# Softmax statistics and joining coefficients of a dilated attention layer: by way of DRAM in place of TensorE

## The chip, the cores and the metric

The kernel runs on one core of one Trainium2 chip. The metric is the device time of one execution in microseconds (us). The kernel before was timed three times: median 1245.1 us, lowest 1243.75, highest 1247.14. One further execution was profiled and took 1243.98 us, of which the profile's span covers 1242.2 us. TensorE is PE below, VectorE DVE, ScalarE ACT, GpSimd POOL, and SyncE, which issues most transfers, SP.

## The reference

A trunk of two layers over 512 tokens of width 1024. Layer A (sparse attention and memory attention, then an MLP) is untouched. In layer B each of 8 heads attends three times over shared keys and values, in windows (128, step 1), (512, step 4) and (2048, step 16), and the three results are merged by their softmax denominators:

```python
for gi, (window, dil) in enumerate(DIL_PATTERNS):
    n_k = window // dil + 1
    idx = t[:, None] - dil * jnp.arange(n_k)[None, :]
    s = jnp.einsum('bhqd,bhqkd->bhqk', q_b[:, gi], k_g).astype(jnp.float32) * scale
    s = jnp.where(valid, s, NEG)
    lse = jax.nn.logsumexp(s, axis=-1, keepdims=True)
    p = jnp.exp(s - lse)
    outs.append(jnp.einsum('bhqk,bhqkd->bhqd', p.astype(v.dtype), v_g))
    lses.append(lse)
wts = jax.nn.softmax(jnp.stack(lses), axis=0).astype(v.dtype)
return jnp.sum(jnp.stack(outs) * wts, axis=0)
```

The result goes through an output projection and an MLP to the output.

## The kernel before, in words

The heads are worked on in four pairs (`sp` 0 to 3, pair 0 to pair 3 below). For each pair `proj_b` makes the queries: products of 128x384 in float32r, three to a term (lines 275, 279 and 280, helper `mm3`), since each operand is split into a high part and a remainder. The weights come by a transfer into `st`, ACT copies the high part into `w` (line 268), DVE subtracts for the remainder (line 270); line 275 multiplies by the high part, line 279 by the remainder. `attn_b` then has two rounds `w`. Round 0 is the local window (step 1), with queries in natural order. Round 1 is the two dilated windows together (steps 4 and 16), with queries sorted by residue modulo 4. In each round the scores (line 790) go to PSUM, DVE adds the mask and takes the running minimum of the negated scores (line 754, "mask" below), ACT takes the exponential (line 231), PE turns the probabilities (lines 1676 and 1685), and PE multiplies them with the values (line 771; `close0` ends round 0, `close1` round 1). Both write their 128x512 result to the one PSUM bank of pool `po`. `close0` copies it away in residue order (line 1703, ACT); the result `O1` of `close1` stays in the bank until `norm_b` has read it, so `close0` of the next pair waits for that.

`norm_b` joins the two rounds. The statistics of a round are, for each token and head, a minimum and a sum: `st0` (round 0) and `st1` (round 1), tiles of 128 x 4 blocks x 4 numbers. `st0` has tokens in natural order and must be brought into residue order. Before, PE turns its four blocks to 4x512 (line 1725), DVE copies that with the permutation (line 1727), PE turns it back (line 1731), and DVE copies it out (line 1733). A short chain of DVE operations and one exponential make the coefficients `cc`, two for each token and head. They must be spread from one number for a token and head to 64 partitions: DVE splits them (lines 315 and 316), PE turns them to 8x512 (line 1755), DVE copies (line 1759), and PE spreads them by two products with a matrix `sel` of ones (lines 1763 and 1768). ACT copies one of the two out (line 1765), DVE multiplies (lines 1766 and 1769), adds (line 1770) and splits the sum for the output projection (lines 1774 and 1775).

What sets the order: `norm_b` is a generator in a side queue; each `yield` hands one step of `attend`, which puts one item of attention work and some projection work between, and the counts NY, NZ (before: 6 and 0) say how many steps to pause. A scheduler then fixes the order on each engine from this sequence; each engine works strictly in that order, and an instruction that waits holds all behind it. The same holds for the order in which SP issues transfers.

## Time and profile before

| | |
|---|---|
| median of 3 runs | 1245.1 us (1243.75 to 1247.14) |
| profiled execution | 1243.98 us, span 1242.2 us |
| busy, share of the span | PE 1221.2 us (98%), DVE 821.2 (66%), ACT 720.5 (58%), POOL 331.0 (27%) |
| attention of layer B, with its side work | about 727 to 895 us of the span |
| first and last instruction of line 1725 (start of `norm_b` on PE) | 770.7 and 864.4 us |
| last product with `sel` (line 1768) | 880.1 us |

In rows of a timeline the columns are start and duration in us, engine, line, operation, output and inputs, and count; a bracket gives the idle time just before and what ended it. Matmuls are pipelined: the duration of one overlaps the next, so the time that one takes from PE is read from start to start.

### The profile page before, as it was taken

The page shows a single profiled execution, that of the slowest core. Times are in us where ns is not written, and L with a number is a line of the kernel's source. Part 1 is how long each engine was busy: PE and PEld are TensorE (multiplying, and loading weights), DVE is VectorE, ACT ScalarE, POOL GpSimd, SP SyncE. Part 2 cuts the span into 40 slices and gives each one's busy share as a digit, 9 for nine tenths or more (in the row PEclk, how much of TensorE's full clock was granted, in tenths as well). Part 3 has the DMA queues.
Part 4 walks back from the last instruction along what each step waited for, and adds up shares of the span by engine and source line. Part 5 has one row for each costly group of instructions (what it writes and reads, how often), then busy time and mean ns, then how long its engine had stood idle before and what let it go on. Part 6 is the DMA issues. An engine that isn't in the chain of part 4 may idle for free.

```text
span 1242.2 us, 17962 instructions
## 1 busy us (share of the span) xinstructions
PE 1221.2 (98%) x6307; PEld 998.0 (80%) x6307; DVE 821.2 (66%) x1531; ACT 720.5 (58%) x1579; POOL 331.0 (27%) x418
## 2 busy tenths in 40 slices
PE   9999999999999999999999999999999999999998
PEld 7768877787788888888888898877688888888887
DVE  7857676764567557566589566777766747557466
ACT  6834678874476464553557446667666455364462
POOL 4535864731040000000001767642241000000000
PEclk9999999999999999999999999999999999999999
DMA  7531232342498797896976342211379698697634
GB/s 272 203 107 44 96 109 94 89 115 84 131 273 235 227 274 224 266 246 216 275 218 200 97 130 61 70 39 41 124 220 267 212 274 248 200 295 220 170 109 162
DMA packets 62219, 215.41 MB, mean 173 GB/s; under 512 B 6929, under 2 KB 15313, under 8 KB 61617
## 3 DMA queue, kind: packets, MB, share of 16 engines
q1 hardware_dynamic: 50656, 143.69, 35.4%
q0 software_dynamic: 9728, 35.93, 14.8%
q10 hardware_dynamic: 1744, 34.63, 7.5%
q8 instruction: 50, 0.82, 0.3%
q14 instruction: 41, 0.33, 0.1%
HBM read 208.89 MB, written 72.35 MB: 226 GB/s over the span
## 4 chain that ended last, share of the span: by engine, by line
PE 72%; ACT 5%; DVE 5%; POOL 2%; issue 2%; DMA 2%; ACTq 0%; DVEq 0%; POOLq 0%
PE s_ps L275 13%; PE s_ps L279 13%; PE s_ps L280 13%; PE s_acc L275 5%; PE s_acc L280 5%; PE s_acc L279 5%; PE s_pt L280 3%; PE s_pt L275 3%; PE s_pt L279 3%; PE s_po L771 3%; ACT s_p L231 1%; PE s_ps L790 1%; DVE s_w L270 1%; ACT s_pt L767 1%; ACT s_w L268 1%
## 5 line engine op out<-in xcount | busy, mean ns | idle before, releaser
L270 DVE TENSOR_TENSOR s_w<-s_st,s_w 128x1024 fp32r<-128x1024 f32 (+3 forms) x254 | 295.9, 1171 | 252.8 <-ACT s_w L268 252.3
L268 ACT ACTIVATE s_w<-s_st 128x1024 fp32r<-128x1024 f32 (+4 forms) x260 | 251.4, 973 | 211.3 <-PE s_pt L280 54.7
L275 PE MATMUL s_ps<-s_act,s_w 128*128 128x512 f32 x560 | 218.6, 392 | 1.0 <-ACT s_act L313 0.7
L279 PE MATMUL s_ps<-s_act,s_w 128*128 128x512 f32 x560 | 218.3, 390 | 0.0
L280 PE MATMUL s_ps<-s_act,s_w 128*128 128x512 f32 x560 | 218.1, 390 | 0.0
L1238 POOL DMA_DIRECT2D sum<-sum x16 | 14.2, 887 | 430.8 <-ACT s_p L231 430.8
L275 PEld LDWEIGHTS s_ps<-s_act,s_w 128*128 128x128 f32 x560 | 104.9, 188 | 24.0 <-ACT s_act L313 2.0
L279 PEld LDWEIGHTS s_ps<-s_act,s_w 128*128 128x128 f32 x560 | 105.2, 188 | 22.1 <-DVE s_act L316 0.4
L280 PEld LDWEIGHTS s_ps<-s_act,s_w 128*128 128x128 f32 x560 | 105.1, 188 | 21.8
L275 PE MATMUL s_acc<-s_w,s_act 128*128 128x512 f32 (+3 forms) x288 | 102.1, 359 | 2.1 <-ACT s_act L294 0.7
L279 PE MATMUL s_acc<-s_w,s_act 128*128 128x512 f32 (+3 forms) x288 | 101.4, 354 | 0.0
L280 PE MATMUL s_acc<-s_w,s_act 128*128 128x512 f32 (+3 forms) x288 | 99.5, 351 | 0.0
L231 ACT ACTIVATE s_p<-s_ps 128x512 f32<-128x512 f32 x64 | 38.0, 594 | 89.1 <-PE s_ps L280 86.3
L759 POOL TENSOR_SCALAR s_p<-s_p,s_cr,s_ab 128x128 f32<-128x128 f32 (+3 forms) x96 | 61.0, 661 | 58.8 <-DVE s_cr L1127 39.2
L231 ACT ACTIVATE s_p<-s_ps,s_nm 128x256 f32<-128x256 f32 (+3 forms) x128 | 65.8, 528 | 16.0 <-PE s_pt L1145 4.5
L767 ACT ACTIVATE s_pt<-s_pt 128x512 f32<-128x512 f32 (+2 forms) x99 | 51.5, 528 | 20.6 <-PE s_pt L1676 7.3
L275 PEld LDWEIGHTS s_acc<-s_w,s_act 128*128 128x128 f32 x288 | 54.2, 188 | 10.3 <-issue 1.7
L313 ACT ACTIVATE s_qk<-s_p 128x256 fp32r<-128x256 f32 (+1 forms) x96 | 46.9, 489 | 21.2 <-DVE s_p L1248 19.4
L279 PEld LDWEIGHTS s_acc<-s_w,s_act 128*128 128x128 f32 x288 | 54.4, 189 | 4.2 <-issue 0.2
L280 PEld LDWEIGHTS s_acc<-s_w,s_act 128*128 128x128 f32 x288 | 54.1, 189 | 4.4
L316 DVE TENSOR_TENSOR s_qk<-s_p,s_qk 128x256 fp32r<-128x256 f32 (+1 forms) x96 | 50.9, 530 | 0.0
L279 PE MATMUL s_acc<-s_w,s_qk 128*128 128x512 f32 x128 | 49.9, 390 | 0.0
(329 smaller groups left out, 2724.6 us busy)
## 6 DMA issues: line engine op xcount, KB each, us to landing
s_st<-in_w_up_dram SPq DMA_DIRECT2D x64, 512.0 KB, 4.3
s_st<-sum SPq DMA_DIRECT2D x64, 512.0 KB, 6.1
s_st<-in_w_db_dram SPq DMA_DIRECT2D x48, 512.0 KB, 4.4
sum<-in_w_db_dram POOLq DMA_DIRECT2D x16, 1024.0 KB, 14.2
sum<-sum POOLq DMA_DIRECT2D x16, 1024.0 KB, 11.2
s_st<-in_w_bq_dram SPq DMA_DIRECT2D x16, 384.0 KB, 3.4
s_st<-in_w_ag_dram SPq DMA_DIRECT2D x11, 512.0 KB, 3.6
s_w<-in_w_c_dram SPq DMA_DIRECT2D x8, 512.0 KB, 4.7
```

Of the source, the lines that this page charges most:

```text
L231: return lambda *a, **k: self.marks.append(f(*a, **k))
L268: nc.scalar.activation(w[:, 0], st, AF.Copy)
L270: e.tensor_tensor(out=w[:, 1], in0=st, in1=w[:, 0], op=ALU.subtract)
L275: m = mm(ps, lh[0], rh[0], start=start, stop=False, skip_group_check=again)
L279: mm(ps, lh[0], rh[1], start=False, stop=False, skip_group_check=again)
L280: mm(ps, lh[1], rh[0], start=False, stop=stop, skip_group_check=again)
L313: nc.scalar.activation(dst[:, 0], src, AF.Copy)
L316: nc.vector.tensor_tensor(out=dst[:, 1], in0=src, in1=dst[:, 0], op=ALU.subtract)
L759: self.nc.gpsimd.tensor_scalar(out=p, in0=p, scalar1=c, scalar2=g, op0=ALU.mult, op1=ALU.mult)
L767: self.turned = self.nc.scalar.activation(dst, src, AF.Copy)
L771: i = self.nc.tensor.matmul(*a, **k)
L1238: self.behind(self.nc.gpsimd.dma_start(t[o], x, accum_op=ALU.add, max_dma_last_dim=4096))
```

## The change

The reordering of `st0` and the spreading of the coefficients go through DRAM. In `close0`, once the round-0 statistics are complete, SP writes `st0` to a DRAM tile `sd` in natural order and reads it back in residue order (tile `s0`). In `norm_b` the four turns by line 1725 and four by line 1731 and their copies go. The coefficients are laid out as 16 columns and PE turns them once, to 16x128; DVE copies that; SP writes it to a DRAM tile `cd`, and four transfers read it back, each one row of 512 numbers to 64 partitions, two for each product, those for the dilated round first. Then come five pauses (NX), and DVE multiplies from these two tiles. One pause (NE) stands behind the exponential; NY and NZ become 0 and 1. The split of the coefficients, the turns to 8x512, the products with `sel` and ACT's copy go, and so does `sel` in the constants, which shrink from 768 to 512 columns.

```diff
-NY, NZ = 6, 0
+NY, NZ, NX, NE = 0, 1, 5, 1
...
-        m = self.t("st", [P, 768])
+        m = self.t("st", [P, 512])
         nc.sync.dma_start(m, self.ins["c1"])
-        c1 = self.t("ab", [P, 768], F32R)
-        nc.vector.tensor_copy(c1, m)
+        c1 = self.t("ab", [P, 256], F32R)
+        nc.vector.tensor_copy(c1, m[:, 256:512])
...
             nc.scalar.activation(a.rearrange("p (r u) -> p r u", r=4), self.perm(O), AF.Copy)
-            acc.append(a)
+            s0 = self.t("stt", [P, NB, 4])
+            sd = self.dram.tile([S, 4], F32, name=f"sd{sp}")
+            nc.sync.dma_start(sd.rearrange("(b p) c -> p b c", p=P), st0)
+            nc.sync.dma_start(s0, sd.rearrange("(u r) c -> u r c", r=4))
+            acc.extend((a, s0))
...
-        pt = self.ps(self.pT, [4, S])
-        for b in range(NB):
-            nc.tensor.transpose(pt[:, b * P : (b + 1) * P], st0[:, b, :], self.idf)
-        row = self.t("p2", [4, S])
-        nc.vector.tensor_copy(row.rearrange("p (r u) -> p r u", r=4), self.perm(pt))
-        yield
-        pt = self.ps(self.pT, [P, NB, 4])
-        for r_ in range(NB):
-            nc.tensor.transpose(pt[:, r_, :], row[:, r_ * P : (r_ + 1) * P], self.idf[0:4, 0:4])
-        s0 = self.t("stt", [P, NB, 4])
-        nc.vector.tensor_copy(s0, pt)
-        yield
...
         nc.scalar.activation(ee, ee, AF.Exp)
+        for _ in range(NE):
+            yield
...
-        ch = self.t("nb", [P, NB, 2, 4], F32R)
-        self.split(ch.rearrange("p r t c -> p t r c"), cc.rearrange("p r w s -> p r (w s)"), "v")
         for _ in range(NY):
             yield
-        pt = self.ps(self.pT, [8, S])
-        for r_ in range(NB):
-            nc.tensor.transpose(
-                pt[:, r_ * P : (r_ + 1) * P].bitcast(F32R), ch[:, r_].rearrange("p t c -> p (t c)"), self.idr
-            )
-        rows = self.t("p2", [8, S], F32R)
-        nc.vector.tensor_copy(rows, pt)
+        pt = self.ps(self.pT, [4 * NB, P])
+        nc.tensor.transpose(pt, cc.rearrange("p w s r -> p (w s r)"), self.idf)
+        row = self.t("p2", [4 * NB, P])
+        nc.vector.tensor_copy(row, pt)
+        cd = self.dram.tile([2, 2, S], F32, name=f"cd{sp}")
+        nc.sync.dma_start(cd.rearrange("w s (r u) -> (w s r) u", u=P), row)
         for _ in range(NZ):
             yield
-        pc = self.ps(self.pT, [P, S])
-        nc.tensor.matmul(pc, self.sel[:, 1, :], rows, start=True, stop=True)
-        cb = self.t("p2", [P, S])
-        nc.scalar.activation(cb, pc, AF.Copy)
-        nc.vector.tensor_tensor(out=cb, in0=O1, in1=cb, op=ALU.mult)
-        pc = self.ps(self.pT, [P, S])
-        nc.tensor.matmul(pc, self.sel[:, 0, :], rows, start=True, stop=True)
-        nc.vector.tensor_tensor(out=acc, in0=acc, in1=pc, op=ALU.mult)
+        cb = [None, None]
+        for w_ in (1, 0):
+            c = self.t("p2", [P, S])
+            for s_ in range(2):
+                d = cd[w_, s_ : s_ + 1, :]
+                nc.sync.dma_start(
+                    c[64 * s_ : 64 * s_ + 64, :],
+                    bass.AP(tensor=d.tensor, offset=d.offset, ap=[[0, 64], [1, S]]),
+                )
+            cb[w_] = c
+        for _ in range(NX):
+            yield
+        nc.vector.tensor_tensor(out=cb[1], in0=O1, in1=cb[1], op=ALU.mult)
+        nc.vector.tensor_tensor(out=acc, in0=acc, in1=cb[0], op=ALU.mult)
+        cb = cb[1]
         nc.vector.tensor_tensor(out=acc, in0=acc, in1=cb, op=ALU.add)
```

The lines of the changed kernel stand one lower from line 470 on, so that line 754 before is line 753, line 771 is 770, line 790 is 789, line 1676 is 1675 and line 1685 is 1684. The new lines are 1705 and 1706 (statistics out and back), 1727 to 1741 (the chain of coefficients), 1745 and 1747 (the turn and its copy), 1749 and 1757 (coefficients out and back), and 1764, 1765, 1767 (the two products and the sum) and 1771, 1772 (the split of it).

The order on PE where `norm_b` of pair 0 begins, with `s_acc` a projection of pair 2. Before:

```order
L1685 MATMUL s_pt_7712<-c_118,s_p_1635_7506 128x128 x2
...
L1725 MATMUL s_pt_7751<-c_118,s_stt_7306 4x128 x4
L275 MATMUL s_acc_7912<-s_w_7681,s_act_7020 128x384
...
L1731 MATMUL s_pt_7777<-c_118,s_p_1694_7756 128x4 x4
L1676 MATMUL s_pt_7842<-c_118,s_p_1683_7706 128x128 x3
L1685 MATMUL s_pt_7738<-c_118,s_p_1636_7512 128x128 x2
```

In the change:

```order
L1684 MATMUL s_pt_7716<-c_118,s_p_1636_7510 128x128 x2
...
L1745 MATMUL s_pt_7788<-c_118,s_nb_7785 16x128
L275 MATMUL s_acc_7911<-s_w_7685,s_act_7020 128x384
...
L1675 MATMUL s_pt_7816<-c_118,s_p_1683_7705 128x128 x3
L1684 MATMUL s_pt_7742<-c_118,s_p_1637_7516 128x128 x2
```

The one turn of finished coefficients stands where the four turns of raw statistics stood, and the second set is gone.

The order on DVE a little later, from the last mask of pair 1, round 0, to the first remainder of the weights of pair 3 (`s_w`, line 270). Before:

```order
L754 ISA s_ps_7762,s_stt_7308<-s_ps_7762,bm 128x256
...
L1536 TENSOR_TENSOR s_tq_8007<-s_acc_7912,gr 128x384
L529 TENSOR_REDUCE s_r_1753_8011<-s_sq_8009 128x6
L270 TENSOR_TENSOR s_w_8111<-s_st_8109,s_w_8111 128x768
L535 SCALAR_TENSOR_TENSOR s_r_1755_8017<-s_r_1753_8011,et,s_r_1754_8013 128x6
L754 ISA s_ps_7860,s_stt_7309<-s_ps_7860,bm 128x256
```

In the change:

```order
L1747 COPY s_p_1703_7790<-s_pt_7788 16x128
L1535 TENSOR_TENSOR s_tq_7997<-s_acc_7911,gr 128x384
L1764 TENSOR_TENSOR s_p_1713_7821<-s_po_7746,s_p_1713_7821 128x512
L528 TENSOR_REDUCE s_r_1749_8001<-s_sq_7999 128x6
L753 ISA s_ps_7859,s_stt_7309<-s_ps_7859,bm 128x256
...
L1765 TENSOR_TENSOR s_raw_7482<-s_raw_7482,s_p_1714_7824 128x512
...
L1767 TENSOR_TENSOR s_raw_7482<-s_raw_7482,s_p_1713_7821 128x512
...
L1771 CAST s_act_7918<-s_raw_7482 128x512
L270 TENSOR_TENSOR s_w_8101<-s_st_8099,s_w_8101 128x768
```

The copy of the turned coefficients now stands behind the masks of pair 1, the product that reads them back (line 1764) only one instruction behind that copy, and the first remainder of the weights has moved from ahead of the next masks to behind the products.

The order on SP at the same place. Before:

```order
L1595 DMA s_x_8100<-vd 32x4x128 x4
L249 DMA s_st_8109<-in_w_bq_dram 128x768
L249 DMA s_st_8114<-in_w_bq_dram 128x768
L249 DMA s_st_8146<-in_w_bq_dram 128x768
L1597 DMA s_x_8105<-vd 128x4x128
L249 DMA s_st_8157<-in_w_bq_dram 128x768
```

In the change:

```order
L249 DMA s_st_8136<-in_w_bq_dram 128x768
L1749 DMA cd_7792<-s_p_1703_7790 16x128
L1757 DMA s_p_1713_7821<-cd_7792 64x512 x2
L1757 DMA s_p_1714_7824<-cd_7792 64x512 x2
L1705 DMA sd_7942<-s_stt_7308 128x4x4
L1596 DMA s_x_8095<-vd 128x4x128
L1706 DMA s_stt_7941<-sd_7942 128x16
L249 DMA s_st_8147<-in_w_bq_dram 128x768
```

Seven transfers have come in ahead of the last weight piece of pair 3 (`in_w_bq`); the reads wait on SP for the write of `cd` to land, the read of `sd` for its write.

More of the change, by code (lines that the diff above doesn't have):

```diff
@@ L465, in setup_b @@
         nc = self.nc
[L466 removed]
+        m = self.t("st", [P, 512])
         nc.sync.dma_start(m, self.ins["c1"])
[L468 to L469 removed]
+        c1 = self.t("ab", [P, 256], F32R)
+        nc.vector.tensor_copy(c1, m[:, 256:512])
         self.bm = self.c("bm", [P, 512])
[L471 to L473 removed]
+        nc.vector.tensor_copy(self.bm, m)
+        self.bm12 = c1.rearrange("p (a b) -> p a b", a=2)
     def square(self, m, x, e=None):
@@ L1714, in close1, with norm_b @@
                     )
-            side.add(self.norm_b(st0, st1, acc[0], O, oT))
+            side.add(self.norm_b(sp, acc[1], st1, acc[0], O, oT))
         order = [(s, w, ih) for w in range(2) for ih in range(2) for s in range(2)]
         return [Item(front, back, a, sp, sp or None, 2 * sp + a[1]) for a in order]
-    def norm_b(self, st0, st1, acc, O1, oT):
+    def norm_b(self, sp, s0, st1, acc, O1, oT):
         nc = self.nc
-        pt = self.ps(self.pT, [4, S])
-        for b in range(NB):
-            nc.tensor.transpose(pt[:, b * P : (b + 1) * P], st0[:, b, :], self.idf)
-        row = self.t("p2", [4, S])
-        nc.vector.tensor_copy(row.rearrange("p (r u) -> p r u", r=4), self.perm(pt))
-        yield
-        pt = self.ps(self.pT, [P, NB, 4])
-        for r_ in range(NB):
-            nc.tensor.transpose(pt[:, r_, :], row[:, r_ * P : (r_ + 1) * P], self.idf[0:4, 0:4])
-        s0 = self.t("stt", [P, NB, 4])
-        nc.vector.tensor_copy(s0, pt)
-        yield
         m = self.t("nb", [P, NB, 2])
@@ L1817, in constants @@
     ok2 = (kk <= q) & (kk % 4 == q % 4)
-    sel = np.zeros((P, 2, P), np.float32)
-    for w in range(2):
-        for part in range(2):
-            for s in range(2):
-                sel[part * 4 + w * 2 + s, w, s * 64 : s * 64 + 64] = 1.0
-    return a, np.concatenate([neg(kb >= q), neg(kb <= q), caus, neg(ok2), sel.reshape(P, 256)], axis=1)
+    return a, np.concatenate([neg(kb >= q), neg(kb <= q), caus, neg(ok2)], axis=1)
 def layout(inp):
```

7 lines of the change are left out of this document (2 added, 5 removed).

## The prediction

> **What bounds the kernel now.** I read the page's table of engines first, then busy time by stretch where the change acts, then PE's waits there.
>
> ```profile
> PE 1221.2 (98%) x6307; PEld 998.0 (80%) x6307; DVE 821.2 (66%) x1531; ACT 720.5 (58%) x1579; POOL 331.0 (27%) x418
> ```
>
> PE is busy for 98% of the span: a microsecond taken from its queue counts unless PE then waits. By stretch (PE's busy time is the second figure after the bounds; clock, DMA share and GB/s end the row):
>
> ```profile
> 760.00:780.00 20.00, 19.56 (x132) 16.39 (x130) 14.75 (x51) 10.84 (x43) 13.64 (x15) 1.00 0.19 60
> 780.00:800.00 20.00, 18.90 (x140) 16.03 (x141) 15.42 (x39) 15.65 (x53) 12.61 (x13) 1.00 0.33 109
> 800.00:820.00 20.00, 20.00 (x147) 17.15 (x143) 12.59 (x49) 13.52 (x48) 11.58 (x13) 1.00 0.05 14
> 820.00:840.00 20.00, 18.37 (x147) 15.21 (x148) 18.46 (x50) 12.30 (x50) 9.06 (x9) 1.00 0.16 47
> 840.00:860.00 20.00, 19.29 (x158) 15.09 (x156) 14.91 (x54) 15.67 (x55) 6.37 (x9) 1.00 0.05 14
> 860.00:880.00 20.00, 19.70 (x131) 16.32 (x130) 15.98 (x41) 13.69 (x40) 6.68 (x13) 1.00 0.38 116
> ```
>
> In these 120 us PE is idle for 120 less 115.8, about 4.2 us. The clock stays at 1.00, and the DMA engines are mostly free (0.05 to 0.38). The longest waits between 760 and 890 us are short, and none of them is for the joining itself:
>
> ```profile
> PE s_pt L1547 <- POOL s_tq L1542: 1.1, 1, 1.1
> PE s_ps L790 <- DVE s_qk L1588: 0.9, 1, 0.9
> ```
>
> **What the change removes from PE.** The price is from start to start, here for pair 0:
>
> ```profile
> 770.68 0.60 PE L1725 MATMUL s_pt<-c,s_stt 128*4 128x128 f32 x4
> 771.04 0.43 PE L275 MATMUL s_acc<-s_w,s_act 128*128 128x384 f32 x1
> ...
> 773.44 0.41 PE L1731 MATMUL s_pt<-c,s_p 4*128 4x4 f32 x4
> 773.78 0.55 PE L1676 MATMUL s_pt<-c,s_p 128*128 128x128 f32 x3
> ...
> 781.87 1.16 PE L790 MATMUL s_ps<-s_qk,s_qk 64*128 64x128 f32 x14
> 782.96 1.09 PE L1676 MATMUL s_pt<-c,s_p 128*128 128x128 f32 x8
> 783.80 0.48 PE L1755 MATMUL s_pt<-idr,s_nb 128*8 128x128 f32 x4
> 784.12 0.39 PE L275 MATMUL s_acc<-s_w,s_act 128*128 128x384 f32 x1
> ...
> 787.92 0.49 PE L1763 MATMUL s_pt<-s_p,s_ab 8*128 8x512 f32 x1
> 788.25 0.39 PE L1768 MATMUL s_pt<-s_p,s_ab 8*128 8x512 f32 x1
> 788.58 0.55 PE L1547 MATMUL s_pt<-c,s_tq 128*128 128x128 f32 x3
> ```
>
> Line 1725 takes 0.36, line 1731 0.34, line 1755 0.32, and lines 1763 and 1768 together 0.66: 1.68 us, for four pairs 6.7. The one turn that is added is of the kind of line 1725, a quarter of 0.36, so 0.1 each and 0.4 in all. **PE's work shrinks by 6.3 us.** ACT loses a copy of 128x512 for each pair and DVE three copies and a split; neither bounds, so these count for nothing, and the narrower cast of the constants, ahead of all this on DVE, too.
>
> **What it adds: two hops through DRAM.** The trace has no transfer of this size, so the bounds come from the nearest rows (the last figure is us from issue to landing; the row below them is for the 64 KB reads of `vd`):
>
> ```profile
> xd<-s_x SPq DMA_DIRECT2D x8, 256.0 KB, 4.3
> out_dram<-s_pt SPq DMA_DIRECT2D x8, 256.0 KB, 2.0
> s_x<-vd SPq DMA_DIRECT2D x16, 64.0 KB, 2.8
> ```
> ```profile
> DMA to landing us min/median/max: 2.0/2.8/4.8
> ```
>
> A write of 256 KB takes 2.0 us (the output) or 4.3 (`xd`); a read from DRAM 2.0 to 4.8. With 0.4 for the second read's issue, a hop takes 4.4 us at the least and 9.5 at the most. I take 2.0 + 0.4 + 2.8 = 5.2, since these stretches are quiet.
>
> [...]
>
> The hop of the statistics is hidden: those of pair 0 are complete on ACT, and needed on DVE, at
>
> ```profile
> 745.81 0.21 ACT L231 ACTIVATION_READ_ACCUMULATOR s_p<-s_ps,s_stt 128x1 f32 x1
> ```
> ```profile
> 760.50 0.14 DVE L754 DVE_READ_ACCUMULATOR2_ANT s_stt<- 128x1 f32 x1
> ```
>
> That leaves 14.7 us for at most 9.5. What covers it is the dilated round of the same pair; without that cover each pair would pay the hop. On SP the read of `sd` waits for its write to land, and the loads behind it by as much; the nearest, the last weight piece of pair 3, needs a buffer that DVE's line 270 frees later anyway.
>
> The hop of the coefficients is the open one. The product of line 1764 stands on DVE's queue almost at once behind the copy of line 1747, so DVE waits out the hop. Behind it stand the masks of pair 1's dilated round, the other products, and the remainder (line 270) of the first weight of pair 3, for which PE's line 279 waits. I walk both queues from the last local scores of pair 1:
>
> ```profile
> 774.47 1.14 PE L790 MATMUL s_ps<-s_qk,s_qk 64*128 64x256 f32 x8
> 775.54 0.44 PE L275 MATMUL s_acc<-s_w,s_act 128*128 128x384 f32 x1
> ...
> 777.98 1.09 PE L771 MATMUL s_po<-s_pt,s_x 128*64 128x128 f32 x16
> 779.00 0.55 PE L1676 MATMUL s_pt<-c,s_p 128*128 128x128 f32 x3
> ...
> 785.05 0.33 PE L280 MATMUL s_acc<-s_w,s_act 128*128 128x384 f32 x1
> ...
> 787.13 0.33 PE L280 MATMUL s_acc<-s_w,s_act 128*128 128x384 f32 x1
> ...
> 794.80 1.74 PE L771 MATMUL s_po<-s_pt,s_x 128*64 128x256 f32 x16
> 796.46 0.33 PE L1587 MATMUL s_pt<-c,s_x 128*128 128x128 f32 x1
> ```
> ```profile
> L754 DVE CUSTOM_DVE_ANT_0 s_ps<-s_ps,bm x60: 286/433/489, 742.7 to 857.0; 128x256 f32<-128x256 f32 x54, 128x128 f32<-128x128 f32 x6
> ```
> ```profile
> L270 DVE TENSOR_TENSOR s_w<-s_st,s_w x5: 950/959/1339, 763.0 to 791.3; 128x768 fp32r<-128x768 f32 x5
> ```
> ```profile
> L1766 DVE TENSOR_TENSOR s_p<-s_po,s_p x4: 679/682/687, 792.2 to 881.3; 128x512 f32<-128x512 f32 x4
> ```
>
> PE: those scores end at 775.5, with 0.6 saved ahead of them 774.9. Up to line 279's first product with pair 3's remainder stand, in the new order, 36 products of 384 columns (12 of them took 787.13 less 785.05, so 0.173 each, 6.2), 17 turns (eight took 783.80 less 782.96, 0.105 each, 1.8), 17 scores of 128 columns (14 took 1.09; 1.3), `close1` (1.0) and `close0` (1.7): 12.0, so PE is there at 786.9.
>
> DVE: the four masks (0.43 each) follow the scores as they come and end near 776.4; the copy is small, 776.6; the hop ends at 781.8. Then eleven instructions: two products and a sum (0.7 each), four more masks (1.7), the first half of the split (0.7), line 270 (0.96), and three small ones (about 1 us): 6.5, less some 0.08 of overlap at each, so about 5.7. That is 787.5: **PE stalls for 0.6 us** (none with the hop at its least, 4.9 with it at its most). Pair 1 has slack: its masks are done when `close0` of pair 2 still lies ahead, and I charge nothing (up to 3 at the most). In pair 2 the masks of pair 3's dilated round stand behind the product, with about even timing: 0.5 (0 to 4.5). Pair 3 has some 2 us of slack before the last part of the output projection: nothing (up to 2).
>
> **Sum**: 6.3 less 1.1 is 5.2 us gained. From the profiled execution's 1243.98 us that is 1238.8; the median of the runs lies 1.1 above this execution, so **1239.9 us**.
>
> **Rivals.** (1) *The freed time comes back as other waits.* What PE drops was also filler: at the wait for POOL's line 1542 above, PE would only come earlier to the same wait. Against it, those chains start from PE's own products and move forward with them. For it, DVE now stands idle about 5 us for each pair, in which it did the work that feeds ACT and POOL. If each pair gives back 1.2 to 1.5 us, about 5 to 6 in all, instead of 0.3, the time is near 1244.5, no change. (2) *The hop is slow, and DVE's held queue decides: slower.* From a hop of about 4.6 us on, each further one delays pair 0's remainder, and so PE, by as much. At 9.5 the four bounds above add to 4.9 + 3 + 4.5 + 2 = 14.4, less 6.3: 8.1 slower, 1253. For it speaks the 4.3 us write; against it the idle DMA engines. [...] (3) *More is gained*: the two waits of 1.1 and 0.9 vanish with the new order and the hop is short, 6.3 + 1 or so, 1238.
>
> **How the numbers follow.** The forecast gets 0.53, rival 1 0.27, rival 2 0.13, rival 3 0.07. A measurement of this kernel tells 0.3%, 3.7 us, from no change. Of the forecast about 0.85 lies beyond that (below 1241.4); with rival 3, 0.52 for faster. Rival 1 and the rest of the forecast make 0.33 for no change; rival 2 and the tail of rival 1 0.15 for slower. The forecast's own range is 1237.5 to 1243; the range for 8 in 10 reaches from rival 3 with margin, 1236.5, over rival 1 to 1247.5, and leaves rival 2 out.
>
> **What would show it.** Right: no line of `norm_b` on PE but the turn of 16 columns; PE busy in the joining stage down by about 6 us; DVE idle ahead of line 1764 for 4 to 5 us in each pair, released by a DMA, with the reads landing in 2 to 3 us; PE waiting for under 1.5 us on line 270 and line 753 behind it. Wrong: waits of PE at line 279 or 790 of several us, reads that land 4 us or later, DVE waiting at line 1727 for the statistics, or SP's weight loads late for ACT. What would undo the forecast most is a DVE that, held for the hop, starves ACT and POOL at more places than the two that I priced.

## The result, and the profile after

The changed kernel takes 1253.08 us (median of four runs, 1251.42 to 1254.84) against 1245.05 us before (four runs, 1243.75 to 1247.14): a ratio of 1.0068, 95% interval 1.0056 to 1.0080, **8.0 us slower**. I had forecast 5.2 us faster. The profiled execution took 1251.42 us, its span is 1249.5 us, against 1242.2 before.

First the page's table of engines, after the change; PE's busy time is what it was, though 52 matmuls have gone.

```profile
PE 1221.2 (98%) x6255; PEld 999.0 (80%) x6255; DVE 815.9 (65%) x1515; ACT 718.7 (58%) x1575; POOL 337.0 (27%) x418
```

The loss can be placed by one instruction that stands in both: behind the attention of layer B, the first products of the MLP wait 0.70 us for the same work of ACT. Before, then after:

```profile
891.99 0.73 PE L275 MATMUL s_ps<-s_act,s_w 128*128 128x512 f32 x2 [0.70 <-ACT s_act L313]
```
```profile
899.45 0.73 PE L275 MATMUL s_ps<-s_act,s_w 128*128 128x512 f32 x2 [0.70 <-ACT s_act L313]
```

It comes 7.46 us later, and the whole span is 7.3 longer: all of the loss lies in the joining stage. The stage itself is 8.3 us longer, because at one and the same turn of query terms ahead of it (line 1547, 1546 in the changed kernel) the changed kernel is 0.87 us earlier, 756.92 against 757.79. That is no gain of the change: e5 below, in which nothing is removed, is as early there, 756.80. Busy time by stretch from this turn to the start of the wait above, before and after (bounds, length, busy time of PE, of the weight loads, DVE, ACT and POOL, then clock, DMA share, GB/s):

```profile
757.79:891.29 133.50, 129.31 (x909) 104.81 (x907) 102.12 (x300) 89.56 (x306) 63.82 (x73) 1.00 0.22 69
```
```profile
756.92:898.75 141.83, 129.78 (x857) 105.81 (x855) 96.36 (x283) 88.10 (x302) 69.37 (x74) 0.95 0.29 79
...
780.00:800.00 20.00, 18.46 (x122) 15.71 (x120) 17.93 (x45) 13.19 (x44) 15.64 (x13) 0.91 0.46 130
...
820.00:840.00 20.00, 15.06 (x102) 13.33 (x103) 16.84 (x46) 13.33 (x46) 14.23 (x13) 0.83 0.16 47
```

PE's idle time is 133.50 less 129.31, 4.19, before and 141.83 less 129.78, 12.05, after: **7.9 us more waiting**. Its busy time rose by 0.47 us, where the removed work should have taken 6.3 off, so the work that is left took **6.8 us longer**. The clock accounts for that: it was 1.00 in all these stretches before and is 0.95 over the whole of the stage now, and 0.05 of 141.83 is 7.1. Together 7.9 and 0.5 make the 8.3.

What PE waits for, by groups (us in all, times, the longest), in the attention of layer B:

```profile
PE s_pt L1684 <- POOL s_p L1664: 5.9, 4, 3.2
PE s_pt L706 <- POOL s_p L758: 2.2, 2, 1.6
```

That is POOL, which the prediction did not walk. ACT, too, waits longer for DVE: its exponentials stand for the masks for 15.9 us in ten waits, against 4.9 in five before.

How the hop gets to POOL and PE is seen in pair 1, on DVE, POOL and PE (start, duration; in the bracket the idle time before and what ended it):

```profile
807.95 0.27 DVE L1747 COPY s_p<-s_pt 16x128 f32<-16x128 f32 x1
...
813.35 0.69 DVE L1764 TENSOR_TENSOR s_p<-s_po,s_p 128x512 f32<-128x512 f32 x1 [5.06 <-DMA s_p<-cd]
816.28 0.69 DVE L1765 TENSOR_TENSOR s_raw<-s_raw,s_p 128x512 f32<-128x512 f32 x1 [2.24 <-DMA s_p<-cd]
...
818.94 0.56 DVE L1535 TENSOR_TENSOR s_tq<-s_acc,gr 128x384 f32<-128x384 f32 x1
```
```profile
819.58 1.41 POOL L547 TENSOR_TENSOR s_rb<-s_tq,c 128x384 f32<-128x384 f32 x1 [10.31 <-DVE s_tq L1535]
820.95 1.44 POOL L1664 TENSOR_TENSOR s_p<-s_p 128x256 f32<-128x256 f32 x1
822.35 1.97 POOL L548 TENSOR_TENSOR s_tq<-s_tq,c 128x384 f32<-128x384 f32 x1
824.29 1.70 POOL L1664 TENSOR_TENSOR s_p<-s_p 128x256 f32<-128x256 f32 x1
```
```profile
826.04 0.69 PE L1684 MATMUL s_pt<-c,s_p 128*128 128x128 f32 x2 [3.16 <-POOL s_p L1664]
```

DVE stands for 5.06 us, does one product, and stands again for 2.24, because the data of the second product land 8.1 us after the copy's end (816.28 less 808.22). Line 1535, behind both, is what POOL has been waiting for, 10.31 us. Not all of this wait is the hop's: before, POOL waits for the same line at the same place, for 5.87 us, and then does the same four instructions, among them the two that add up the probabilities of the dilated windows (line 1665, now 1664):

```profile
815.80 1.02 POOL L548 TENSOR_TENSOR s_rb<-s_tq,c 128x384 f32<-128x384 f32 x1 [5.87 <-DVE s_tq L1536]
816.78 0.73 POOL L1665 TENSOR_TENSOR s_p<-s_p 128x256 f32<-128x256 f32 x1
817.48 1.01 POOL L549 TENSOR_TENSOR s_tq<-s_tq,c 128x384 f32<-128x384 f32 x1
818.46 0.73 POOL L1665 TENSOR_TENSOR s_p<-s_p 128x256 f32<-128x256 f32 x1
```

Counted from the turn ahead of the stage, these four now start 4.65 us later (819.58 less 756.92, against 815.80 less 757.79), and they take 6.41 us in place of 3.39. Beside them DVE now works off lines 1771, 1772 and 270 (819.41 to 826.40), where before it stood idle for 2.09 us, up to 817.81. No run separates whether that is why, and the profile gives its spans on POOL as rough. PE, which turns the sums, waits 3.16 us for the last of them. Behind the wait the clock is low:

```profile
826.00:828.00 2.00, 1.96 (x8) 1.96 (x9) 2.00 (x8) 0.98 (x4) 1.41 (x2) 0.50 0.43 115
...
832.00:834.00 2.00, 2.00 (x19) 2.00 (x18) 1.30 (x5) 1.52 (x7) 1.92 (x3) 1.00 0.38 98
```

This wait is so paid twice: 3.16 us while PE stands, and some 2.6 us more while it works at a clock of 0.50, 0.50 and 0.70 in the three stretches from 826 to 832.

The transfers themselves, from issue to landing (median), and SP's issue of the four reads of pair 1 (start, duration):

```profile
s_p<-cd SPq DMA_DIRECT2D x16, 128.0 KB, 3.2
...
cd<-s_p SPq DMA_DIRECT2D x4, 8.0 KB, 1.4
```
```profile
809.75 2.37 SPq L1757 DMA_DIRECT2D s_p<-cd  x4
```

### The profile page after: what moved, and what is told of

The parts are those of the page before. It is cut to its first block, busy times and chain, and to the rows that moved or that the text cites. A ratio compares the mean times of both kernels' runs of the same rounds, so it can differ in the third digit from the quotient of the medians.

```text
span 1249.5 us, 17914 instructions
## 1 busy us (share of the span) xinstructions
PE 1221.2 (98%) x6255; PEld 999.0 (80%) x6255; DVE 815.9 (65%) x1515; ACT 718.7 (58%) x1575; POOL 337.0 (27%) x418
## 3 DMA queue, kind: packets, MB, share of 16 engines
q0 software_dynamic: 9728, 35.93, 14.7%
## 4 chain that ended last, share of the span: by engine, by line
PE 75%; DVE 4%; ACT 4%; DMA 2%; issue 2%; POOL 1%; SPq 0%; ACTq 0%; DVEq 0%; POOLq 0%
PE s_ps L275 14%; PE s_ps L279 14%; PE s_ps L280 14%; PE s_acc L275 5%; PE s_acc L279 5%; PE s_acc L280 5%; PE s_pt L275 3%; PE s_pt L280 3%; PE s_pt L279 3%; PE s_po L770 2%; ACT s_p L231 2%; ACT s_pt L766 1%; DMA s_p<-cd 1%; DMA s_st<-in_w_mem_dram 1%; PE s_ps L1115 1%
## 5 line engine op out<-in xcount | busy, mean ns | idle before, releaser
L275 PEld LDWEIGHTS s_acc<-s_w,s_act 128*128 128x128 f32 x288 | 55.1, 191 | 10.1 <-issue 2.5
L279 PEld LDWEIGHTS s_acc<-s_w,s_act 128*128 128x128 f32 x288 | 55.1, 191 | 4.4 <-issue 0.2
L280 PEld LDWEIGHTS s_acc<-s_w,s_act 128*128 128x128 f32 x288 | 55.0, 192 | 4.1
```

The lines of the kernel that those rows point to most:

```text
L275: m = mm(ps, lh[0], rh[0], start=start, stop=False, skip_group_check=again)
L279: mm(ps, lh[0], rh[1], start=False, stop=False, skip_group_check=again)
L280: mm(ps, lh[1], rh[0], start=False, stop=stop, skip_group_check=again)
```

## The experiments

Every run was timed beside the kernel before on the same chip; the ratio is to that, with its 95% interval.

| run | median, us | ratio |
|---|---|---|
| the change | 1253.08 | 1.0068 [1.0056, 1.0080] |
| e1 statistics half alone | 1253.07 | 1.0084 [1.0069, 1.0099] |
| e2 coefficients half alone | 1257.46 | 1.0114 [1.0101, 1.0127] |
| e3 products with ones | 1251.63 | 1.0067 [1.0050, 1.0083] |
| e4 products behind the masks | 1249.69 | 1.0048 [1.0036, 1.0060] |
| e5 before, with the statistics' transfers unused | 1243.27 | 0.9994 [0.9985, 1.0003] |
| e6 before, NY 2 | 1258.62 | 1.0118 [1.0104, 1.0132] |
| e7 the change, four pauses ahead | 1258.02 | 1.0117 [1.0103, 1.0131] |
| e8 the change, 6.4 us more work for PE | 1254.35 | 1.0080 [1.0067, 1.0092] |
| e9 the change in nearly the old order | 1263.28 | 1.0159 [1.0145, 1.0173] |
| e10 the old work in the change's order | 1268.17 | 1.0194 [1.0179, 1.0208] |
| e11 statistics half, nearly the old order | 1253.53 | 1.0081 [1.0069, 1.0094] |
| e12 before, NY 7 | 1252.00 | 1.0076 [1.0063, 1.0088] |
| e13 statistics half, its own chain tied too | 1251.81 | 1.0061 [1.0047, 1.0075] |
| e14 the change, its own chain tied too | 1268.70 | 1.0201 [1.0185, 1.0218] |
| e15 statistics half, exactly the old order | 1243.00 | 0.9990 [0.9981, 0.9999] |
| e16 the change, exactly the old order | 1256.06 | 1.0104 [1.0089, 1.0120] |
| e17 as e16, the coefficients' hop earlier | 1266.01 | 1.0170 [1.0151, 1.0188] |

### Each half by itself (e1, e2)

My theory after the trace: DVE, held for the coefficients, starves POOL. Then the half with the statistics, in which DVE is held for nothing, should be no slower than before.

```diff
# e1: close0 sends st0 to sd and reads s0 back, norm_b drops
#     lines 1725 to 1733; the coefficients are spread as before
-        pt = self.ps(self.pT, [4, S])
-        for b in range(NB):
-            nc.tensor.transpose(pt[:, b * P : (b + 1) * P], st0[:, b, :], self.idf)
...
# e2: norm_b turns the statistics as before; the coefficients go by cd,
#     with NY, NZ, NX, NE = 0, 1, 5, 1
```

> The kernel before with one half of the change: the local statistics go through DRAM, the coefficients stay on TensorE. PE loses eight turns per pair (0.36 + 0.34 us by the rows of before), 2.8 us in all. Theory A (what costs time in the changed kernel is VectorE standing in its queue for the coefficients' reads, and what is then late): this half has no such wait, granted clock 1.00 in all stretches, about 1242.3 us, between 1241 and 1244. Rival B (PE's removed work was filler; whatever is removed there comes back as PE waits in front of POOL's and ACT's results, and as slow clock): 1245 or more, with new PE waits at the turns of line 1676 or 1685. Rival C (the statistics' transfers hold SP's queue, so that weights come late): slower than before, 1247 or more, with ACT waiting for weight pieces at line 268.

> The kernel before with the other half: the coefficients go through DRAM with the pauses of the change, the statistics stay on TensorE. PE loses 0.98 us per pair and gains 0.1, 3.5 us in all. Theory A: VectorE waits 3 us or more per pair for the reads, PE stands still 1.5 to 4 us at a stretch at line 1684's turn, the granted clock falls below 0.9 in at least two stretches of 20 us: 1252 to 1257 us. Rival B: also above 1245, but no worse than the change, with PE gaps that do not follow a held VectorE. Rival C: no loss, about 1241.5.

Both halves are slower alone, by 0.84% and 1.14%, and together they cost no more than the cheaper one. Two prices that don't add, and a half that loses without any hop in DVE's way: the theory does not cover e1, and something that both edits touch is at work. PE's waits in e1 are several small ones, none for the joining. One of them, 1.12 us at line 1547 at 799.23, the kernel before had too, 1.10 at 799.06. Busy time in the stage, from the same turn ahead of it to the wait for the MLP:

```profile
756.24:899.02 142.78, 133.12 (x877) 106.40 (x875) 99.66 (x291) 90.07 (x306) 65.39 (x74) 0.98 0.22 63
```

PE's idle time is 142.78 less 133.12, 9.66, against 4.19, 5.5 more; and its busy time has grown by 3.8 where the eight turns of each pair (0.70) should have taken 2.8 off, so the work that is left took 6.6 us longer. The clock accounts for about half of that: it is 0.91, 0.98 and 0.94 in three of the stretches of 20 us from 760 on, and 1.00 in the others, some 3.4 us. What made the rest is not shown.

### The hop by itself (e3, e4)

```diff
# e3: both products take a resident tile of ones
-        nc.vector.tensor_tensor(out=cb[1], in0=O1, in1=cb[1], op=ALU.mult)
-        nc.vector.tensor_tensor(out=acc, in0=acc, in1=cb[0], op=ALU.mult)
+        nc.vector.tensor_tensor(out=cb[1], in0=O1, in1=self.unit, op=ALU.mult)
+        nc.vector.tensor_tensor(out=acc, in0=acc, in1=self.unit, op=ALU.mult)
# e4: both products may only come behind the last mask issued ahead of them
+            self.together_dep(i, self.mask, "products behind the masks")
```

> The changed kernel, but the two products multiply by a resident tile of ones; the coefficients are still written to DRAM and read back by the same transfers, and nothing reads what lands. So the joining coefficients are left out of the result; VectorE's wait for the reads goes, all of PE's work is as in the changed kernel. Theory A: VectorE no longer idle ahead of the first product, PE's waits at lines 1684 and 706 shrink to what the kernel before had (under 1.5 us each place), clock 1.00, 1237 to 1241 us. Rival B: PE still runs ahead of POOL and ACT, 1249 to 1254 us. Rival C (SP's queue): 1249 to 1254 us with late weights.

> The changed kernel with one thing more: both products are tied behind the four masks (or the maximum) given out last, so that VectorE does those first and comes to the products some nine instructions later; the transfers, the pauses and PE's work are as in the changed kernel. Theory A: VectorE's idle time ahead of the first product falls from 3 to 7 us to under 1.5 us in pairs 0 and 1, POOL's half-sum of line 1664 is no longer late, the PE waits of 1.5 to 3.2 us and the slow clock behind them go: 1238 to 1243 us. If only part of the bunching goes, 1243 to 1248. Rival B: PE's gaps stay, 1250 or more.

In e3 the coefficients are turned and moved but not applied. It does not test what it was made for: the first product still writes into the tile that the reads fill, so DVE waits for them all the same (`[1.95 <-DMA s_p<-cd]` ahead of it in pair 0, and 5.26, 2.37 and 0.81 us in the other pairs), and the second, freed, went elsewhere in the order. At 1.0067 it says nothing either way. In e4 DVE waits for no read longer than 0.90 us in any pair, and the ratio falls from 1.0068 to 1.0048, some 2.5 us, with intervals that just overlap. So DVE's hold is worth a part, and 6 us of loss are left without it.

### The transfers by themselves, and PE's work by itself (e5, e8)

```diff
# e5, in the kernel before: the transfers, their result unused
+            s0 = self.t("stt", [P, NB, 4])
+            sd = self.dram.tile([S, 4], F32, name=f"sd{sp}")
+            nc.sync.dma_start(sd.rearrange("(b p) c -> p b c", p=P), st0)
+            nc.sync.dma_start(s0, sd.rearrange("(u r) c -> u r c", r=4))
# e8, in the change: 18 turns of a constant for each pair, unused
+        self.idle(8)
...
+        self.idle(10)
```

> The kernel before, with the two transfers of the local statistics added and nothing that uses what lands; TensorE still reorders the statistics, and the order of all engines but SP's is as before. Rival C (the transfers themselves cost: SP's queue held, weights late): 1248 us or more, as with the statistics' half alone. Theory D (the transfers are harmless; what costs is that the joining now starts about four masks earlier in VectorE's order, in the stretch where VectorE also splits the next weights): as before, 1244 to 1246 us. Rival B (PE's removed work was filler): as before too.

> The changed kernel, with 18 turns of 128x128 for each pair that nobody reads put on TensorE, at the head of the joining and ahead of the products, about 0.105 us each and 7.6 us in all: a little more work than the change took away. Rival B (the removed work filled what are now PE's waits, and held the clock): not slower than the changed kernel, 1245 to 1252 us, clock 1.00. Theory D or A (PE waits for results that are late whatever it does between): 1256 to 1262 us, the clock lower only where it is now.

e5 leaves the order of every engine as it was, and costs nothing (a ratio of 0.9994): neither the transfers nor the read that waits on SP's queue do harm. e8 puts back about as much work as the change took, 18 turns for each pair, 6.4 us in all when the 72 are measured from start to start (the expectation counts 7.6), and by the ratios is 0.12% slower than the change, some 1.5 us, with intervals that overlap; its time lies between the two that were forecast. In its trace the clock makes up for most of the work: it is 0.91 from 800 to 820 us and 1.00 in the other stretches, 1.8 us lost in place of 6.8. Its order came out differently once more, so this is no clean price of the work.

### The order by itself (e6, e7, e12)

What e1 and e2 share is that the sequence from which the order is fixed has other work in it, and so the order of everything else comes out differently, on all engines. If that is the price, a change of the order alone must cost as much.

```diff
# e6, e12: the kernel before, with another count of pauses
-NY, NZ = 6, 0
+NY, NZ = 2, 0          # e12: 7, 0
# e7: the change, norm_b begins with four pauses
+        for _ in range(4):
+            yield
```

> The kernel before with NY 2 in place of 6: the same work on every engine, no transfer more, but the copy of the coefficients comes four masks earlier in VectorE's order in pairs 0 and 2 (after mask 24 in place of 28, and 56 to 60), and the products with it. Theory D: slower than before by 2 to 8 us, 1246 to 1252, with PE waits behind POOL or VectorE and clock below 1.00 in one of the stretches 780 to 840. Rivals B and C: no work is removed and no transfer added, so as before, 1244 to 1246 us.

> The kernel before with NY 7 in place of 6: the same work, and an order that differs little (places elsewhere on TensorE 1252; NY 2, which took 1258.6 us, has 6414). Order theory: close to before, 1243 to 1249 us, slower the more instructions moved. Hold and filler theories: as before, 1243 to 1246.

> The changed kernel with four pauses more at the head of the joining, so that copy, transfers and products stand where they stood before in VectorE's order (copy after masks 28, 44 and 60, products after 30, 44 and 60); all transfers and all removed work as in the changed kernel. Theory D: most of the loss goes, 1238 to 1245 us, clock 1.00 in all or all but one stretch. Theory A (VectorE held for the reads, wherever that is): 1248 to 1254, since the product still stands close behind the copy. Rival B: 1249 to 1254.

Two different orders of the same instructions cost 1.18% and 0.76%. One pause more, of six, is worth as much as the whole change. In e6 PE stands longest for a joining turn that now comes ahead of its operands, the line 316 of the split. In e12 the largest group of waits (us in all, times, the longest) is also one of the joining, for the copy of line 1759. So part of the price is the joining's own place:

```profile
890.57 0.59 PE L1755 MATMUL s_pt<-idr,s_nb 128*8 128x128 f32 x4 [4.73 <-DVE s_nb L316]
```
```profile
PE s_pt L1763 <- DVE s_p L1759: 3.8, 3, 2.2
```

Both took more than was forecast for a change of the order (1246 to 1252 us for e6, 1243 to 1249 for e12). How many instructions change their place does not tell the price: by the expectation they are 6414 on PE in e6 and 1252 in e12, and e12 costs two thirds of e6.

e7 does not help the change: with the chain later, PE meets other waits, the longest 5.17 us for a copy of DVE.

### The old order put back (e9 to e14)

If the order is the price, the change in the old order must give its gain. The order was put back by hand, with a list of pairs of instructions for each engine, of which the second may not come ahead of the first (here from e9):

```diff
+TIES = {
+    "PE": [
+        (3121, 3110), (3156, 3139), (3161, 3142), (3183, 3167), (3185, 3147), (3189, 3173), (3175, 3150), (3621, 3731), (3690, 3758),
...
+            for x, y in ties:
+                self.tc.add_manual_dep(
+                    i[y], i[x].name, mybir.DependencyInfo(mybir.DependencyClass.NoSync, mybir.DependencyReason.DATA),
```

> The work of the changed kernel (all transfers, all removed work; pauses 2 at the head, NY 6, no others), with 114 ties between instructions outside the joining that put TensorE, VectorE, ScalarE and GpSimd back into nearly the order of the kernel before: the places by which TensorE's instructions stand elsewhere add up to 732, against 5654 in the changed kernel. Order theory (what costs is the new order of everything else, which the scheduler made when the joining's work changed; the removed work itself is a gain): 1236 to 1241 us, clock 1.00. Hold theory (VectorE waits for the reads, and that costs): 1247 to 1254, since the product still stands soon behind the copy. Filler theory (PE's removed work only comes back as waits): 1243 to 1250.

> The work of the kernel before, nothing through DRAM, NY 6, with 116 ties that put the instructions outside the joining into nearly the order that they have in the changed kernel (places of TensorE's instructions elsewhere: 462, counted against the changed kernel). Order theory: slower than before, 1248 to 1258 us, with PE waits of over 1.5 us behind POOL or VectorE and clock below 1.00 in some stretch of 780 to 900. Hold and filler theories: as before, 1243 to 1246, since no work is removed and nothing waits for a transfer.

> The statistics' half alone (2.8 us of TensorE's work gone), with 64 ties that bring the order back to nearly that of the kernel before (places elsewhere on TensorE 506, against 5518 without ties, where it took 1253.1 us). Order theory: 1239.5 to 1243 us. Filler theory: 1244 to 1248, since waits come back. If a transfer's wait cost here: above 1248.

> The statistics' half alone, as in the run that took 1253.5 us, and now the joining's own instructions tied to their old places too: its chain starts on VectorE after masks 20, 40, 52 and 64 as before (there after 16, 32, 48 and 64). VectorE's and GpSimd's orders are those of the kernel before to the last instruction, TensorE's differ in five short pieces. Chain theory (an early chain holds the projection's norm, POOL's line 1542 comes late and PE waits 2 to 8 us at line 1547): 1240 to 1244 us, the 2.8 us saved or most of it, clock 1.00. If order and chain are not the cause: 1249 to 1255 as in the run before. Filler theory: 1244 to 1247.

> All of the change's work, with the joining's own instructions tied to their old places too, the product with the tile that lands first at the earlier of the two old product places. The chain starts after masks 20, 40, 48 and 64, the products stand 4 and 6 us behind the copy. Chain theory: 1238 to 1245 us, the gain of 6.3 less what VectorE still waits for the reads (1 to 3 us a pair at most). If not: 1250 to 1264, as in the run before.

These were the misses that mattered. e10, the old work tied into nearly the new order, is slower by 1.94%, more than the change; but so are e9 and e14, the change in nearly the old order, with 1.6% and 2.0%; and e11 is no better than e1. Taken alone they speak against the theory. The trace of e13 shows why "nearly" doesn't do. There DVE and POOL keep the old order exactly, and PE's differs in five short pieces. One of them, in pair 2, before (line 1547, a turn of query terms that come from POOL's line 1542) and in e13 (the same turn, line 1566):

```profile
833.55 0.70 PE L790 MATMUL s_ps<-s_qk,s_qk 64*128 64x256 f32 x4 [0.93 <-DVE s_qk L1588]
834.18 0.44 PE L1685 MATMUL s_pt<-c,s_p 128*128 128x128 f32 x2
...
836.02 0.49 PE L1547 MATMUL s_pt<-c,s_tq 128*128 128x128 f32 x3
```
```profile
835.65 0.86 PE L1566 MATMUL s_pt<-c,s_tq 128*128 128x128 f32 x3 [2.72 <-POOL s_tq L1561]
836.30 0.42 PE L1606 MATMUL s_pt<-c,s_x 128*128 128x128 f32 x1
...
842.63 0.69 PE L1704 MATMUL s_pt<-c,s_p 128*128 128x128 f32 x2 [3.16 <-ACT s_qk L1569]
```

Before, scores and other turns stand ahead of this turn, and it comes unwaited. In e13 it has come ahead of them, and PE, which works strictly in order, stands for 2.72 us; a turn that it has overtaken (line 1606, before 1587, at 831.43) runs unwaited behind it. Its own three instructions then take 0.65 us (836.30 less 835.65), with the clock at 0.50 in the stretch from 836 to 838; they took 0.32 before. A few places on the queue, that is all. The longest wait is of another kind. The turn of probabilities at 842.63 stands 3.16 us for ACT's line 1569, which does not make its operands but reads another PSUM tile of the same pool: PE waits for the buffer. The turns take the two PSUM buffers of their pool in rotation, and where a group of turns is removed, every later user gets another buffer, freed by other work than before. That is also why these pieces could not be tied back. So an order and a rotation have changed, and which of the two costs how much in e1 is not told apart; the next runs put both back at once.

### Exactly the old order (e15, e16, e17)

So in these three a product of 4x4 that nobody reads stands in for each removed group of turns, only to keep the rotation. With it PE, DVE, ACT and POOL hold exactly the old order in e15 and e16; in e17 the coefficients' turn, copy and transfers come ahead of the six pauses and not behind them.

```diff
+    def spot(self, shape):
+        pt = self.ps(self.pT, shape)
+        pt = pt[0:4, 0:4] if len(shape) == 2 else pt[0:4, 0, :]
+        self.nc.tensor.matmul(pt, self.idf[:, 0:4], self.idf[:, 0:4], start=True, stop=True)
...
+        self.spot([4, S])
+        yield
+        self.spot([P, NB, 4])
+        yield
# e17, against e16
-        for _ in range(NY):
-            yield
         pt = self.ps(self.pT, [4 * NB, P])
...
+        for _ in range(NY):
+            yield
         nc.vector.tensor_tensor(out=cb[1], in0=O1, in1=cb[1], op=ALU.mult)
```

> The statistics' half alone: eight turns per pair replaced by two products of 4 x 4 numbers that nobody reads, everything else on TensorE, VectorE, ScalarE and GpSimd in exactly the order of the kernel before. Order theory: the removed work comes out as a gain, 0.70 less about 0.1 for each pair, 2.4 us in all: 1240 to 1242.5 us, clock 1.00. Filler theory (the waits grow by what goes): 1243 to 1246. If neither order nor filler is the cause: 1250 as in the last run.

> All of the change, with four such small products per pair, in exactly the order of the kernel before. TensorE's work shrinks by 6.3 less about 0.8 us. The products stand where they stood, 4 to 6 us behind the copy in pairs 0 and 1, but at once behind it in pair 2, so VectorE must wait about 5 us there and up to 2 in pair 3. Order theory: 1238 to 1243 us, with the wait of pair 2 showing on VectorE and costing TensorE up to 4. Hold theory (any VectorE wait for the reads costs as seen in the changed kernel): 1246 to 1253. If the order is not the cause: 1260 or more, as in the last run.

> As the run in exactly the old order that took 1256.1 us, all of the change's work, with one thing moved: the coefficients' turn, copy, write and reads go ahead of the six pauses, so the copy comes after masks 24, 40, 56 and 64 and the products stay after 28, 46, 60 and 64. Two more products of 4 x 4 numbers for each pair keep the turn at the PSUM buffers; TensorE's order is otherwise exactly that of the kernel before, VectorE's and ScalarE's differ by single places around the chain. If the order and VectorE's wait for the reads are the whole of the loss: VectorE waits under 1 us ahead of the products in pairs 0 to 2, TensorE's waits over 1.5 us go, clock 1.00, 1237 to 1242 us (5.2 us of work saved, up to 4 given back where the turn now stands ahead of its operands). If something else of the coefficients' half costs (the transfers themselves, the buffers that the two tiles hold): 1248 to 1257.

**e15 settles where the loss of the statistics' half comes from.** The same half that cost 0.84% in the order that it was given costs nothing in the old one, with the old rotation: the ratio is 0.10% in its favour (0.01 to 0.19%), 1.3 us. PE's waits are those of before (1.2 and 0.9 us), the clock is 1.00, and in the stage PE's idle time is 133.12 less 128.74, 4.38, as against 4.19:

```profile
757.19:890.31 133.12, 128.74 (x893) 102.93 (x891) 99.30 (x292) 89.33 (x306) 63.22 (x73) 1.00 0.24 69
```

Whether it gains is at the edge of what these runs can tell: e5, in which nothing is removed, is 0.06% in front itself, and 2.4 us were expected. The stand-ins cost more than the 0.1 us for each pair that were allowed for them. In pair 0 PE saves 0.13 and 0.21 us where the groups took 0.36 and 0.34, so some 1.4 us in four pairs and not 2.8, and in the trace the stage is 0.4 us shorter (133.12 for 133.50).

**e16 shows that the coefficients have a price of their own**, 1.04% with PE, DVE, ACT and POOL in the old order. DVE's longest hold (copy, first product), and PE's waits of over 1.5 us:

```profile
854.12 0.28 DVE L1810 COPY s_p<-s_pt 16x128 f32<-16x128 f32 x1 [0.58 <-PE s_pt L1809]
859.66 0.69 DVE L1829 TENSOR_TENSOR s_p<-s_po,s_p 128x512 f32<-128x512 f32 x1 [5.26 <-DMA s_p<-cd]
```
```profile
799.72 0.62 PE L1568 MATMUL s_pt<-c,s_tq 128*128 128x128 f32 x3 [3.61 <-POOL s_tq L1563]
...
831.71 0.33 PE L1608 MATMUL s_pt<-c,s_x 128*128 128x128 f32 x1 [2.15 <-ACT s_qk L1571]
...
860.40 2.22 PE L792 MATMUL s_po<-s_pt,s_x 128*64 128x256 f32 x16 [2.50 <-DVE s_p L1829]
...
891.56 1.94 PE L792 MATMUL s_po<-s_pt,s_tmp 128*64 128x512 f32 x8 [1.69 <-DVE s_p L1829]
```

From the end of the copy to the product it is 5.3 us in pair 2 (859.66 less 854.40). In pairs 2 and 3 (the last two rows) PE waits for the product itself, which frees the one bank of `po`. The other two come by other ways.

In pair 0 PE waits for POOL, 3.61 us, where before it waited 1.10 (the first fence; the second is DVE in e16):

```profile
799.06 0.55 PE L1547 MATMUL s_pt<-c,s_tq 128*128 128x128 f32 x3 [1.10 <-POOL s_tq L1542]
```
```profile
791.53 1.50 DVE L1830 TENSOR_TENSOR s_raw<-s_raw,s_p 128x512 f32<-128x512 f32 x1
...
794.15 1.37 DVE L1832 TENSOR_TENSOR s_raw<-s_raw,s_p 128x512 f32<-128x512 f32 x1
```

POOL waits there for DVE's line 557, and from the weight remainders ahead of the products to that line DVE takes 2.6 us longer than before. The hold of the first product is 1.2 of that (`[1.21 <-DMA s_p<-cd]`). The other 1.4 are the second product and the sum (the second fence): they took 0.68 and 0.81 before, when the second factor came from PSUM. POOL works beside them (790.83 to 794.98); in the other pairs the second product takes 0.69, in pair 1 with POOL idle.

In pair 1 DVE waits only 0.50 us for the reads, but SP's queue, whose order was not put back, has a price. SP issues the four reads and only then the next load of output weights, at 825.12, where before it did so at 822.24. ACT stands 4.22 us for these weights, 1.72 before, and the reading of query terms for which PE waits 2.15 us (line 1571) stands behind it on ACT's queue:

```profile
822.08 2.37 SPq L1820 DMA_DIRECT2D s_p<-cd  x4
...
825.12 0.43 SPq L271 DMA_DIRECT2D s_st<-in_w_bo_dram  x1
```
```profile
828.54 0.52 ACT L290 ACTIVATE s_w<-s_st 128x384 fp32r<-128x384 f32 x1 [4.22 <-DMA s_st<-in_w_bo_dram]
```

So the coefficients are paid for in three ways: by the hold, by what DVE does next, and on SP. 1256.06 us lies above the 1246 to 1253 that were forecast for the hold alone.

**e17** gives the hop its room, and DVE no longer waits for a DMA in it. It needs seven stand-ins for each pair, three more than e16. But now the turn is early for its operands, and PE stands for DVE's chain in every pair, 9.7 us in all, 4.03 in pair 0, 2.75 in pair 2 and 2.53 in pair 3. At 1266 us it is slower than either forecast for it:

```profile
777.58 0.37 PE L1813 MATMUL s_pt<-c,s_nb 128*16 128x128 f32 x1 [4.03 <-DVE s_nb L1811]
...
856.13 0.37 PE L1813 MATMUL s_pt<-c,s_nb 128*16 128x128 f32 x1 [2.75 <-DVE s_nb L1811]
```

Whether a place between the two, behind the chain and 6 us ahead of the products, would pay, stays open. It wasn't tried: with the turn at such a place the rotation of the buffers moves again, and with it the order.

## Why the prediction was wrong

**"PE's work shrinks by 6.3 us": right as a count, and worth almost nothing.** 6307 matmuls became 6255, which are the 13 for each pair that it counts. Where the order is held (e15), the stand-ins leave some 1.4 of the 2.8 us in it, and what arrives, 1.3 us by the ratio and 0.4 in the trace, is at the edge of what can be told. In the order that the change really got, 6.4 us of work can be added for some 1.5 (e8), where the clock takes 5 us less than in the change.

Two steps failed. How the 8.3 us of the stage divide between them is not known, since the two halves of the change don't add.

**The first is one that came without a number**: the sum takes the order of everything outside the joining as it was, and so books the 6.3 us as time. "Those chains start from PE's own products and move forward with them", it says against the first rival; they do not, since the scheduler made a new order from a sequence with other work in it. In this kernel PE's queue has little slack at the turns of query terms: in pair 2 before, POOL's line 1542 is done at 834.27, in the row below, and the turn starts at 836.02, 1.75 us later; in pair 0 there is none, and PE waits 1.10. A few places on the queue use that up.

```profile
833.44 0.83 POOL L1542 TENSOR_TENSOR s_tq<-s_tq,s_r 128x384 f32<-128x384 f32 x1 [0.37 <-DVE s_r L536]
```

The statistics half, which has no hop in DVE's way, measures this by itself: 0.84% slower in the new order and rotation, 0.10% faster in the old, about 11.7 us between the two. e6 and e12, with the work unchanged, give 14.7 and 9.5 us, a part of it at the joining's own turns.

**The second is the price of the coefficients' hop**, 1.1 us in the sum. Its length was right, nearly: 5.2 us were forecast from the end of the copy to the product; 5.05 were measured in pair 0, 5.1 in pair 1 (813.35 less 808.22), 6.8 in pair 2 and 6.2 in pair 3. The write is shorter than its row (1.4 us for 2.0), the reads longer (3.2 for 2.8). What I left out is that four reads are issued one behind the other, 0.59 us each, for the one 0.4 in my sum, and that the second product has its own wait: 8.1 us behind the copy in pair 1, close to my upper bound of 9.5.

**The walk of pair 0: the place was right, the waits are not there.** PE does not wait for lines 270 or 753 at all; it waits for POOL. **"Pair 1 has slack ... and I charge nothing (up to 3 at the most)"** is the worst of the four: this is where DVE is held for 7.3 us, POOL stands for 10.31 (5.87 before), and PE loses 3.16 us and then clock. I asked when DVE's masks would be late for PE, and not who else stands behind the hold on DVE's queue: line 1535, the first link of POOL's chain. The last sentence of the prediction names this mechanism, a DVE that starves ACT and POOL, and gives it no price; rival 1 gives it 1.2 to 1.5 us for each pair. With the order of PE, DVE, ACT and POOL in place (e16) the coefficients cost some 14 us against e15, 3.5 for each pair. So the forecast would not have held in the old order either.

**The statistics' hop: right.** e5 shows the transfers free (0.9994), and DVE never waits at line 1727. **SP's queue: nearly right** for the query weights, for which ACT waits once, 0.80 us at 790.48. The output weights, which come behind them, were not asked about: ACT waits 4.5 us for them in two waits, 2.1 in three before, and e16 shows what such a wait can cost.

**The rivals.** Rival 2 had the size, 8.1 us slower, by luck, since its mechanism is not the one: the hop was not slow, and its bounds on lines 279 and 753 are not where the time went. Rival 1 had the mechanism of the hop, too small. None had the price of a new order; rival 3 counts on one, for a gain.

**The clock** was in no term. Before, it is 1.00 in every stretch of this stage, and my sum prices a wait at its length. After, 6.8 of the 14.7 us that PE lost (7.9 of idle time, 6.8 of slower work) are clock.

## What to carry to other kernels

Where a scheduler fixes the order, work that is taken away changes the order of all that is left: time the same work in two or three other orders first, and judge an edit smaller than that spread (here 9 to 15 us) only with the order, and the rotation of buffers, held. On a queue that is full to 98%, ask of each in-order wait not who needs the waiting instruction, but who needs what stands behind it, on every engine. Work off an engine's queue gains time only if the next thing on that queue is ready: here 6.3 us of work went, and 7.9 us of waiting came.

## What the runs showed of the hardware

PE's granted clock fell behind short waits. In the change, PE's last product ahead of a wait of 1.54 us starts at 788.42, the next instruction at 790.29, and the clock is 0.56 and 0.59 in the two stretches behind it (0.50 from 791 to 793, by single microseconds), back to 1.00 at 794.

```profile
788.42 0.34 PE L280 MATMUL s_acc<-s_w,s_act 128*128 128x384 f32 x1
790.29 0.69 PE L1684 MATMUL s_pt<-c,s_p 128*128 128x128 f32 x2 [1.54 <-POOL s_p L1664]
```
```profile
790.00:792.00 2.00, 1.71 (x9) 1.38 (x11) 2.00 (x3) 1.52 (x5) 2.00 (x3) 0.56 0.71 174
792.00:794.00 2.00, 2.00 (x17) 1.78 (x16) 1.65 (x5) 0.75 (x5) 1.92 (x2) 0.59 0.94 338
794.00:796.00 2.00, 2.00 (x14) 2.00 (x13) 1.97 (x8) 1.15 (x4) 1.84 (x3) 1.00 0.56 201
```

It is not a matter of the length alone: in e12 PE stood for 2.48 us, and the clock stayed at 1.00.

```profile
802.34 0.33 PE L1587 MATMUL s_pt<-c,s_x 128*128 128x128 f32 x1 [2.48 <-DVE s_qk L1588]
```
```profile
800.00:802.00 2.00, 0.00 (x0) 0.00 (x0) 2.00 (x3) 0.52 (x3) 1.92 (x2) 1.00 0.25 69
802.00:804.00 2.00, 1.66 (x13) 1.21 (x14) 1.82 (x7) 0.62 (x4) 1.63 (x3) 1.00 0.00 0
```

Some instructions of DVE and POOL took longer in stretches where both engines were at work. In the change POOL's line 1541 takes 2.97 us at 785.87, where DVE runs lines 1771, 270 and 1772, and 0.83 in the eleven other places from 742 us on, also at 827.85 beside DVE's masks; in e16 DVE's line 1830 takes 1.50 with POOL at work and 0.69 with POOL idle. No run separates this from other causes.
